# A hybrid decoder layer: output projection and norm taken in tile order 0, 1, 4, 5, 2, 3, 6, 7, with the residual transfers on SyncE, the token sums on VectorE and the norm's gains folded into the weight rows

## The chip, the cores and the metric

The kernel runs on one core of a Trainium2 chip. The metric is the device time of one execution in microseconds; for the kernel before it is the median of three runs. Five engines work side by side, each through its own list of instructions in order: TensorE (PE, matrix products), VectorE (DVE), ScalarE (ACT), GpSimd (POOL) and SyncE (SP, which only issues transfers here). An instruction waits at the head of its engine's list until what it needs is there, and everything behind it on that engine waits with it.

## The reference, cut to what matters

One layer of a decoder trunk over 1024 tokens of width 1024, all float32. The first half (projections, a state-space mixer, sparse attention, the gated merge `m` of both) is the same in both kernels. What the change touches is the end:

```python
x = x + (g_a * y_a + g_b * y_b) @ w_out[l]          # (1024 x 1024) @ (1024 x 1024)
h = rmsnorm(x, norm_ffn_g[l])
x = x + (jax.nn.silu(h @ w_ffn_gate[l]) * (h @ w_ffn_up[l])) @ w_ffn_down[l]   # 1024 -> 2816 -> 1024
return rmsnorm(x, norm_final_g)
```

## The kernel before

Every float32 operand of a product is split into a high part that TensorE takes at full rate and a low rest (`split`: ACT copies the high part, DVE subtracts), and each product is three matmuls: high by high, high by low, low by high. In the names, `wh`/`wl` are the two parts of a weight tile, `mhi`/`mlo` those of the activations.

**Merge** (`merge`). The 1024 tokens are eight tiles of 128. `w_out` is taken in units of 256 rows by 512 columns (`Weights.next`: the unit in hand has been split, the next is split now, the two behind it are loaded; two raw and three split buffers). A group of tiles shares a unit: tiles 0 to 3 first (four units for the left 512 columns, `q` = 0, and four for the right), then tiles 4 and 5, then 6 and 7, 24 units in all, each loaded and split anew. `add` adds a finished bank to the residual tile `x1`; `norm` squares and sums the row, makes the reciprocal root (`rstd`, ACT and four small DVE instructions), multiplies by it and by the gain row `gffn`, and sends `x1` to DRAM (`xd`). `turn` transposes the tile on PE. Both `x1`'s loads and its stores to `xd` are issued on ACT's queue.

**Feed-forward** (`Winograd`). Each of the 22 matrices (11 of gate, 11 of up, 256 columns each, alternating) is multiplied with the normed activations by Strassen and Winograd's seven products in place of eight, so blocks are needed that are sums of the four quarters: quarters of the contraction (2) by halves of the tokens (tiles 0 to 3, tiles 4 to 7). For the tokens these sums (`t1` to `t4`) are made in `turn` for tiles 4 to 7 against tiles 0 to 3 and kept as `T0` to `T2`; for the weights (`sums`, tile `S`) on POOL, for each matrix. A product is 12 matmuls of 512 columns. Products 1 and 2 need tokens of tiles 0 to 3 only; 3 to 7 need all eight tiles. `early` runs products 1 and 2 of matrices 0 and 1 ahead of `turn(6)` and `turn(7)`, and `run` does the rest. Results go to DRAM (`sd`).

**Down** (`down_loads`, `down`). For each half of the tokens, 22 steps: one loads a piece of the hidden layer back from `sd` (`sr`), splits it (`shi`, `slo`), splits one unit of `w_ffn_down` and does 24 matmuls. `after` is called near the end of the last matrix of `up` and issues the first loads.

The order on each engine is the order in which the Python code emits instructions; buffer counts (`bufs`) decide which of them wait.

## Time and profile before

| what | value |
|---|---|
| median of 3 runs | 1702.38 us (1698.72 to 1703.1) |
| the profiled execution, own time | 1707.91 us |
| its span | 1706.0 us |
| PE busy | 1586.6 us, 93% |
| DVE, ACT, POOL busy | 926.2, 623.7, 564.4 us |

The span is what the engines' records cover; the execution's own time is 1.91 us longer. The profiled execution is 5.5 us above the median of the runs. Merge runs from about 839 to 1009 us, the feed-forward's matrices to 1421 us and the down part from there to the end.

### The profile page before, as it was taken

To read this page: it belongs to the slowest core of one execution; us is meant where nothing else is said; L and a number is where in the kernel's file an instruction comes from. 1 tells how busy PE (TensorE), PEld (TensorE's weight loads), DVE (VectorE), ACT (ScalarE), POOL (GpSimd) and SP (SyncE) were. 2 spreads that over 40 slices of the span, in tenths; PEclk is the share of its full clock that TensorE was granted. 3 is DMA by queue.
4 is the path that set the end of the run, shared out by engine and by line. 5 is a ranking of instruction groups with operands and counts; after the bars stand their busy time and mean duration, and the time that the engine had idled before them with its cause. 6 is when DMAs were issued, how large, how long until landed. Compare 5 with 4: busy or idle time off the path is not lost.

```text
span 1706.0 us, 22111 instructions
## 1 busy us (share of the span) xinstructions
PE 1586.6 (93%) x7868; PEld 1323.6 (78%) x7868; DVE 926.2 (54%) x1735; ACT 623.7 (37%) x1266; POOL 564.4 (33%) x581
## 2 busy tenths in 40 slices
PE   8989999999998999999987659999999996999995
PEld 7667888888886998997765448888888884888884
DVE  7268776412344999997645754444444442335433
ACT  5122334202211898993123333233233331223322
POOL 1037667200120555554300445444544441000001
PEclk9999999999999999999998779999999997999998
DMA  6323443374358411104645211232222214444551
GB/s 211 112 84 109 127 136 90 96 187 115 117 146 265 109 52 47 51 2 134 212 135 192 79 56 56 81 98 87 82 85 87 74 50 131 153 172 159 193 181 60
DMA packets 164773, 196.88 MB, mean 115 GB/s; under 512 B 19770, under 2 KB 118486, under 8 KB 164663
## 3 DMA queue, kind: packets, MB, share of 16 engines
q1 hardware_dynamic: 162359, 187.08, 35.6%
q10 hardware_dynamic: 2304, 8.39, 1.3%
q8 instruction: 63, 1.03, 0.3%
q14 instruction: 47, 0.39, 0.1%
HBM read 145.48 MB, written 47.84 MB: 113 GB/s over the span
## 4 chain that ended last, share of the span: by engine, by line
PE 78%; DVE 8%; DMA 4%; ACT 3%; POOL 2%; issue 2%; SPq 1%; ACTq 0%; POOLq 0%; DVEq 0%
PE a L334 7%; PE a L336 7%; PE a L335 7%; PE a L212 5%; PE a L213 5%; PE a L214 5%; PE O L1241 3%; PE T L1223 3%; PE S L1125 3%; PE b L214 2%; PE b L212 2%; PE b L213 2%; PE a L1521 2%; PE a L1519 2%; PE a L1520 2%
## 5 line engine op out<-in xcount | busy, mean ns | idle before, releaser
L346 DVE TENSOR_TENSOR wl<-wr,wh 128x1024 fp32r<-128x1024 f32 (+1 forms) x170 | 186.2, 1109 | 139.9 <-ACT wh L343 126.9
L334 PE MATMUL a<-hhi,wh 128*128 128x512 f32 x448 | 184.9, 413 | 0.4 <-POOL wh L341 0.4
L343 ACT CAST wh<-wr 128x1024 fp32r<-128x1024 f32 (+1 forms) x138 | 113.4, 842 | 186.8 <-DMA wr<-in_w_out 42.0
L336 PE MATMUL a<-hhi,wl 128*128 128x512 f32 x448 | 178.6, 399 | 2.2 <-DVE wl L346 2.2
L335 PE MATMUL a<-hlo,wh 128*128 128x512 f32 x448 | 178.5, 398 | 0.0
L1196 POOL TENSOR_SCALAR P<-P,sum,gates 128x640 f32<-128x640 f32 (+3 forms) x192 | 124.8, 663 | 116.8 <-DVE sum L1190 70.3
L212 PE MATMUL a<-mhi,wh 128*128 128x512 f32 x352 | 138.0, 392 | 3.7 <-ACT p L225 3.7
L213 PE MATMUL a<-mlo,wh 128*128 128x512 f32 x352 | 137.8, 391 | 0.0
L214 PE MATMUL a<-mhi,wl 128*128 128x512 f32 x352 | 137.5, 391 | 0.0
L1225 DVE TENSOR_TENSOR PTl<-T,PTh 128x512 fp32r<-128x512 f32 (+3 forms) x200 | 104.2, 544 | 10.2 <-ACT PTh L1224 8.7
L341 POOL TENSOR_SCALAR wh<-wr 128x1024 fp32r<-128x1024 f32 x32 | 34.7, 1086 | 216.8 <-PE a L335 163.3
L334 PEld LDWEIGHTS a<-hhi,wh 128*128 128x128 f32 x448 | 85.9, 192 | 25.1 <-issue 6.2
L336 PEld LDWEIGHTS a<-hhi,wl 128*128 128x128 f32 x448 | 85.4, 191 | 22.9 <-DVE wl L346 2.6
L346 DVE TENSOR_TENSOR slo<-sr,shi 128x512 fp32r<-128x512 f32 x44 | 30.4, 691 | 133.3 <-ACT shi L343 133.3
L335 PEld LDWEIGHTS a<-hlo,wh 128*128 128x128 f32 x448 | 85.9, 192 | 17.9
L1176 ACT ACTIVATE P<-P,m 128x640 f32<-128x640 f32 (+7 forms) x128 | 95.8, 748 | 9.1 <-DVE m L1160 9.1
L1224 ACT CAST PTh<-T 128x512 fp32r<-128x512 f32 (+3 forms) x200 | 88.6, 476 | 21.2 <-PE T L1223 20.4
L1160 DVE CUSTOM_DVE_ANT_0 P<-S,B 128x640 f32<-128x640 f32 (+7 forms) x128 | 89.5, 700 | 4.3 <-PE S L1125 2.1
L1223 PE MATMUL T<-cst,P 128*128 128x128 f32 x592 | 87.3, 274 | 3.7 <-DVE PTl L1225 3.1
L343 ACT CAST shi<-sr 128x512 fp32r<-128x512 f32 x44 | 27.3, 620 | 170.0 <-PE c L1520 154.4
L388 POOL TENSOR_SCALAR x1f<-x1f,rstd 128x1024 f32<-128x1024 f32 (+1 forms) x2 | 2.3, 1142 | 251.8 <-DVE rstd L368 246.5
L1519 PE MATMUL a<-wh,shi 128*128 128x512 f32 x176 | 71.0, 403 | 15.4 <-issue 13.6
(411 smaller groups left out, 4017.8 us busy)
## 6 DMA issues: line engine op xcount, KB each, us to landing
wr<-in_w_ffn_down SPq DMA_DIRECT2D x44, 512.0 KB, 3.4
wr<-in_w_in SPq DMA_DIRECT2D x28, 512.0 KB, 4.3
wr<-in_w_out SPq DMA_DIRECT2D x24, 512.0 KB, 5.2
wr<-in_w_ffn_gate SPq DMA_DIRECT2D x22, 512.0 KB, 5.2
wr<-in_w_ffn_up SPq DMA_DIRECT2D x22, 512.0 KB, 4.5
sr<-sd SPq DMA_DIRECT2D x44, 256.0 KB, 3.7
gd<-evf SPq DMA_DIRECT2D x32, 256.0 KB, 2.1
Q<-qd SPq DMA_DIRECT2D x64, 128.0 KB, 3.0
```

What stands on the lines that cost most here:

```text
L212: mm(ps, wh[:, k], bh[:, k], start=first and k == 0, stop=False, skip_group_check=True)
L213: mm(ps, wh[:, k], bl[:, k], start=False, stop=False, skip_group_check=True)
L214: mm(ps, wl[:, k], bh[:, k], start=False, stop=k == 3, skip_group_check=True)
L334: mm(ps, a, c, start=start and k == 0, stop=False, skip_group_check=True)
L335: mm(ps, a, d, start=False, stop=False, skip_group_check=True)
L336: mm(ps, b, c, start=False, stop=stop and k == nk - 1, skip_group_check=True)
L343: nc.scalar.copy(hi, src)
L346: (nc.gpsimd if lo_eng == "pool" else nc.vector).tensor_tensor(lo, src, hi, op=OP.subtract)
L1196: sc = lambda x, y, z: GP.tensor_scalar(x, x, a[:, y:y + 1], gate(z), op0=OP.mult, op1=OP.mult)
L1223: T.transpose(t[:, x, :], p[:, c:c + P], self.ident)
L1225: V.tensor_tensor(ol, t[:, 0:len(cc), :], oh, op=OP.subtract)
L1519: mm(ps, hi[:, t], wh[:, 0, col], start=f == 0, stop=False)
```

## The change

Tiles are taken as 0, 1, 4, 5 (four tiles share each of eight units), then 2, 3, 6, 7 for the left columns (four units), then 2, 3 and 6, 7 apart for the right columns (four units each): 20 units in place of 24. `x1` is loaded and stored from SP. The squares follow the add directly, and a tile's reciprocal root and scaling (now one ACT copy with a scale) come one tile later. The gain vector is no longer multiplied into each row: POOL multiplies it into the weight rows of every matrix (`scale`, eight instructions of 128x256 in place, ahead of `sums`), from a column tile `gcol` (`factors`). The token sums of `turn`, some on POOL before, are on DVE, and for tiles 6 and 7 they are cut into pieces that stand between the products of matrix 0 (`first`). `after` is cut into three steps at earlier places of the last matrix. The core of the diff (`broadcast_row` of `gffn` is dropped, and the old loop of `merge` too):

```diff
+        self.fresh[n] = ts
         self.r[n] = lambda i, k: ts[k - 1][:, :, P * (i - 1):P * i]
+    def scale(self, n):
+        for kh, t in enumerate(self.fresh.pop(n, ())):
+            for k in range(4):
+                self.K.nc.gpsimd.tensor_scalar(t[:, k], t[:, k], self.g[:, 4 * kh + k:4 * kh + k + 1], 1.0,
+                                               op0=OP.mult, op1=OP.mult)
+    def factors(self):
+        self.K.nc.sync.dma_start(self.g, self.K.A["norm_ffn_g"].rearrange("(k p) -> p k", p=P))
+        self.K.nc.gpsimd.tensor_scalar(self.g, self.g, -0.5, 1.0, op0=OP.mult, op1=OP.mult)
...
         if n >= len(self.mats):
             return
+        self.scale(n)
         GP, A = self.K.nc.gpsimd, self.r[n]
...
-    def early(self):
-        self.sums(0)
+    def first(self, turn):
+        V, GP = self.K.nc.vector, self.K.nc.gpsimd
         self.p1(0)
+        self.t2(0)
         self.p1(1)
+        turn("transpose", 6)
+        turn("T1", 6)
         self.p2(0)
+        turn("transpose", 7)
+        turn("T1", 7)
+        self.t3(0)
         self.p2(1)
+        z5, z3, v, y, c = (self.K.bank(t) for t in "aabbc")
+        self.product(0, 5, z5)
+        turn("B22", 6)
+        turn("B22", 7)
+        self.t4(0)
+        self.load(2)
+        self.product(0, 3, z3)
+        turn("T3", 6)
+        turn("T3", 7)
+        self.product(0, 7, v)
+        turn("T2", 6)
+        turn("T2", 7)
+        self.product(0, 6, y)
+        turn("T4", 6)
+        turn("T4", 7)
+        u2, p5, u3 = self.p.pop(0), self.tile("p1"), self.tile("x11")
+        self.K.nc.scalar.copy(p5, z5)
+        V.tensor_tensor(u2, u2, y, op=OP.add)
+        V.tensor_tensor(u3, u2, v, op=OP.add)
+        V.tensor_tensor(u2, u2, z3, op=OP.add)
+        self.sums(1)
+        self.t2(1)
+        self.product(0, 4, c)
+        GP.tensor_tensor(u2, u2, p5, op=OP.add)
+        GP.tensor_tensor(p5, u3, p5, op=OP.add)
+        self.out(0, 1, 1, p5)
+        self.out(0, 0, 1, u2)
+        V.tensor_tensor(u3, u3, c, op=OP.add)
+        self.out(0, 1, 0, u3)
...
+        if last:
+            next(self.after)
         z = K.bank("a")
         self.product(n, 5, z)
         p5 = self.tile("p5")
         AC.copy(p5, z)
-        if n:
-            self.t1(n + 1)
+        self.t1(n + 1)
...
+        self.t2(n + 1)
         if last:
-            self.after()
-        self.t2(n + 1)
+            next(self.after)
         c = K.bank("c")
         self.product(n, 4, c)
...
-        self.t2(0)
-        for n in range(len(self.mats)):
+        for n in range(1, len(self.mats)):
...
         def load(tt):
             x1[tt] = pool.tile([P, D], F32, name="x1", tag="x1", bufs=4)
-            nc.scalar.dma_start(x1[tt], self.A["x"][P * tt:P * tt + P, :])
+            nc.sync.dma_start(x1[tt], self.A["x"][P * tt:P * tt + P, :])
+        def unit(u, q):
+            return self.W.next("w_out", 256 * u, 2, 512 * q, 512, ("act", "dve"))
         def part(w, u, tt, o):
             t = slice(P * tt, P * tt + P)
         def add(tt, q, o):
             x = x1[tt][:, 512 * q:512 * q + 512]
             V.tensor_tensor(x, x, o, op=OP.add)
+            if q:
+                sq[tt] = pool.tile([P, 1], F32, name="ss", tag="ss", bufs=4)
+                xns[tt] = pool.tile([P, D], F32, name="xn", tag="xn", bufs=4)
+                AC.activation(xns[tt], x1[tt], AF.Square, accum_out=sq[tt])
+                nc.sync.dma_start(xd[tt], x1[tt])
         def norm(tt):
-            xns[tt] = self.norm(pool, x1[tt], g, "xn", "dve", 2)
-            nc.scalar.dma_start(xd[tt], x1.pop(tt))
-        def turn(tt):
+            AC.activation(xns[tt], x1.pop(tt), AF.Copy, scale=self.rstd(pool, sq.pop(tt)))
...
+            if what == "T1":
+                pb, pc = (p.rearrange("p (k t) -> p k t", k=4) for p in ps.pop(tt))
+                b22, t1, t3 = tmp[tt] = [pool.tile([P, 4, P], F32, name=n, tag=n, bufs=2)
+                                         for n in ("b22", "t1", "t3")]
+                AC.copy(b22, pc)
+                V.tensor_tensor(t1, pb, first(0, 0), op=OP.subtract)
+                V.tensor_tensor(t1, t1, first(1, 0), op=OP.subtract)
+                V.tensor_tensor(t3, b22, pb, op=OP.subtract)
+                x, o = t1, [x[:, 0:4, at] for x in m]
+            else:
+                b22, t1, t3 = tmp[tt]
+            if what == "B22":
+                x, o = b22, [x[:, 4:8, at] for x in m]
+            elif what == "T3":
+                x, o = t3, [x[:, :, c] for x in td[1]]
+            elif what == "T2":
+                V.tensor_tensor(t1, b22, t1, op=OP.subtract)
+                x, o = t1, [x[:, :, c] for x in td[0]]
+            elif what == "T4":
+                V.tensor_tensor(t3, first(0, 1), t1, op=OP.subtract)
+                V.tensor_tensor(t3, t3, first(1, 1), op=OP.add)
+                x, o = t3, [x[:, :, c] for x in td[2]]
+            self.split(*o, x, "act", "dve")
+        def turned(tt):
             if tt < 4:
                 self.transposed("bc", xns.pop(tt), m[0], m[1], tt)
-                return
-            xs, ps = xns.pop(tt), [self.bank(t) for t in "bc"]
-            for h in range(2):
-                for k in range(4):
-                    nc.tensor.transpose(ps[h][:, k * P:k * P + P], xs[:, (4 * h + k) * P:(4 * h + k + 1) * P],
...
-            V.tensor_tensor(t1, pb, first(0, 0), op=OP.subtract)
-            AC.copy(b22, pc)
-            GP.tensor_tensor(t1, t1, first(1, 0), op=OP.subtract)
-            V.tensor_tensor(t3, b22, pb, op=OP.subtract)
-            GP.tensor_tensor(t2, b22, t1, op=OP.subtract)
-            GP.tensor_tensor(t4, first(0, 1), t2, op=OP.subtract)
-            GP.tensor_tensor(t4, t4, first(1, 1), op=OP.add)
...
+        def units(tts, q, between):
+            banks = [self.bank("a") for _ in tts]
+            for u in range(4):
+                w = unit(u, q)
+                for f, *a in between.get((u, "w"), ()):
+                    f(*a)
+                for i, tt in enumerate(tts):
+                    part(w, u, tt, banks[i])
+                    if u == 3:
+                        add(tt, q, banks[i])
+                        if q and i:
+                            norm(tts[i - 1])
+                for f, *a in between.get(u, ()):
+                    f(*a)
+        units((0, 1, 4, 5), 0, {(0, "w"): [(load, tt) for tt in (0, 1, 4, 5)] + [(ffn.factors,)]})
+        units((0, 1, 4, 5), 1, {3: [(norm, 5)]})
+        units((2, 3, 6, 7), 0, {0: [(turned, 0)], 1: [(turned, 1), (turned, 4)],
+                                (1, "w"): [(load, 2), (load, 3)], (2, "w"): [(load, 6), (load, 7)],
+                                2: [(turned, 5)], (3, "w"): [(ffn.load, 0)], 3: [(ffn.sums, 0)]})
+        units((2, 3), 1, {3: [(norm, 3)]})
+        units((6, 7), 1, {1: [(turned, 2)], (2, "w"): [(ffn.load, 1)], 2: [(turned, 3), (ffn.t1, 0)],
+                          (3, "w"): [(ffn.scale, 1), (ffn.t1, 1)], 3: [(norm, 7)]})
+        ffn.first(turn)
...
         def after():
+            loads[2](2)
             W.until(None)
+            W.ahead(0, 2)
+            yield
+            W.ahead(1, 2)
+            loads[3](1)
+            yield
             W.ahead(2, 4)
-            loads[3](1)
-        ffn.run(after)
+            loads[3](2)
+            yield
+        ffn.run(after())
         for p in (ffn.late, fp, rp, tp, mp):
             p.release()
         pool = self.pool("dn")
```

Three places in the instruction order carry the prediction. The first is ACT at the end of the first group's right columns. Before, tiles 0 to 3 (`x_8706` is tile 0's residual, `xd_8692` its place in DRAM, `x_8992` tile 4's):

```order
L343 CAST wh<-wr 128x1024 x8
L376 ACTIVATE xn,ss<-x_8706 128x1024
L360 ACT_TABLE_LOAD
L360 ACTIVATE rstd<-ss,eps 128x1
L1385 DMA xd_8692<-x_8706 128x1024
L376 ACTIVATE xn,ss<-x_8708 128x1024
L360 ACTIVATE rstd<-ss,eps 128x1
L1385 DMA xd_8693<-x_8708 128x1024
L1369 DMA x_8992<-in_x 128x1024
L1369 DMA x_8994<-in_x 128x1024
L343 CAST wh<-wr 128x1024
```

Now, tiles 0, 1, 4, 5 (`x_8714` to `x_8720`):

```order
L1441 ACTIVATE xn,ss<-x_8714 128x1024
L1441 ACTIVATE xn,ss<-x_8716 128x1024
L413 ACT_TABLE_LOAD
L413 ACTIVATE rstd<-ss,eps 128x1
L1445 ACTIVATE xn<-x_8714,rstd 128x1024
L1441 ACTIVATE xn,ss<-x_8718 128x1024
L413 ACTIVATE rstd<-ss,eps 128x1
L1445 ACTIVATE xn<-x_8716,rstd 128x1024
L1441 ACTIVATE xn,ss<-x_8720 128x1024
L413 ACTIVATE rstd<-ss,eps 128x1
L1445 ACTIVATE xn<-x_8718,rstd 128x1024
L413 ACTIVATE rstd<-ss,eps 128x1
```

The transfers are gone from ACT's list; all four tiles' squares, roots and scaled copies now stand ahead of the next unit's `wh`, where two tiles' squares and roots stood.

The second is SP's list at the last matrix of up and the first down loads. Before (`sd_8688` to `sd_8691` are the last matrix's four results):

```order
L247 DMA sd_8688<-x_12406 128x512
L235 DMA sd_8691<-p_12426 128x512
L235 DMA sd_8689<-p_12378 128x512
L94 DMA wr<-in_w_ffn_down 128x1024 x4
L1469 DMA sr<-sd_8648 128x512
L235 DMA sd_8690<-u_12441 128x512
L351 DMA gfin<-in_norm_final_g 128x1024
L1469 DMA sr<-sd_8650 128x512
```

Now:

```order
L262 DMA sd_8688<-x_12552 128x512
L1523 DMA sr<-sd_8648 128x512
L1523 DMA sr<-sd_8650 128x512
L94 DMA wr<-in_w_ffn_down 128x1024 x2
L250 DMA sd_8691<-p_12580 128x512
L250 DMA sd_8689<-p_12524 128x512
L94 DMA wr<-in_w_ffn_down 128x1024 x2
L250 DMA sd_8690<-u_12603 128x512
L404 DMA gfin<-in_norm_final_g 128x1024
L1523 DMA sr<-sd_8652 128x512
```

The first two pieces of the hidden layer and the first two units of `w_ffn_down` now stand ahead of three of the last matrix's four stores; the third and fourth unit stand between them, and the third piece behind them all.

The third is POOL in the middle of the feed-forward, one matrix of gate. Before (`p_9913` and `u_9934` are its result tiles):

```order
L189 TENSOR_TENSOR S<-wr 128x512
L190 TENSOR_TENSOR S<-S,wr 128x512
L191 TENSOR_TENSOR S<-wr 128x512
L192 TENSOR_TENSOR S<-wr,S 128x512
L279 TENSOR_TENSOR p_9913<-u_9934,p_9913 128x512
```

Now:

```order
L171 TENSOR_SCALAR wr<-wr,gcol 128x256 x8
L204 TENSOR_TENSOR S<-wr 128x512
L205 TENSOR_TENSOR S<-S,wr 128x512
L206 TENSOR_TENSOR S<-wr 128x512
L207 TENSOR_TENSOR S<-wr,S 128x512
L333 TENSOR_TENSOR p_10055<-u_10076,p_10055 128x512
```

Eight instructions are new for each of the 22 matrices, ahead of the four sums.

## Rows read from the trace of the kernel before

**Rows 1.** By stretch: length; busy PE, PEld, DVE, ACT, POOL; PE's clock, DMA share, GB/s.

```profile
876.00:1040.60 164.60, 112.89 (x443) 87.10 (x442) 99.02 (x124) 61.19 (x94) 48.23 (x32) 0.84 0.33 107
1041.00:1421.40 380.40, 380.40 (x1679) 314.78 (x1678) 160.75 (x188) 116.90 (x177) 170.86 (x127) 1.00 0.25 78
1421.40:1452.00 30.60, 15.21 (x50) 11.38 (x50) 8.08 (x9) 6.49 (x9) 2.32 (x2) 0.72 0.57 188
```

**Rows 2.** Waits of PE, 876 to 1041 us: releaser, total us, times, longest.

```profile
PE a L1375 <- ACT wh L343: 23.2, 6, 5.8
PE b L212 <- ACT wh L343: 16.1, 1, 16.1
PE a L1376 <- DVE wl L346: 7.3, 8, 2.0
```

**Rows 3.** PE's timeline: start, us, line, tiles, [idle before <- releaser].

```profile
845.34 0.39 PE L1375 MATMUL a<-wh,mhi 128*128 128x512 f32 x1
...
875.96 0.39 PE L1375 MATMUL a<-wh,mhi 128*128 128x512 f32 x1
...
883.84 0.60 PE L397 MATMUL b<-cst,xn 128*128 128x128 f32 x4
...
1009.22 0.80 PE L212 MATMUL b<-T0h,wh 128*128 128x512 f32 x1 [16.11 <-ACT wh L343]
...
1014.91 0.63 PE L212 MATMUL a<-mhi,wh 128*128 128x512 f32 x1
```

**Rows 4.** ACT by shape, 870 to 1010 us: busy, mean ns | idle before, releasers.

```profile
L343 ACT CAST wh<-wr 128x1024 fp32r<-128x1024 f32 x16 | 16.5, 1047 | 29.3 <-DMA xd<-x 13.0 <-DMA wr<-in_w_out 12.2 <-PE a L1377 3.9
L376 ACT ACTIVATE xn<-x 128x1024 f32<-128x1024 f32 x8 | 8.5, 1062 | 17.7 <-DVE x L1381 17.7
...
L360 ACT ACTIVATE rstd<-ss,eps 128x1 f32<-128x1 f32 x8 | 2.4, 295 | 0.2
...
L360 ACT ACT_TABLE_LOAD x1 | 1.3, 1283 | 0.0
```

**Rows 5.** DVE by shape, 870 to 1010 us, columns as in group 4.

```profile
L1381 DVE TENSOR_TENSOR x<-x,a 128x512 f32<-128x512 f32 x12 | 8.1, 684 | 8.7 <-PE a L1377 8.6
L346 DVE TENSOR_TENSOR T1l<-t,T1h 128x512 fp32r<-128x512 f32 x4 | 7.0, 1752 | 0.0
...
L402 DVE TENSOR_TENSOR mlo<-b,mhi 128x512 fp32r<-128x512 f32 x4 | 2.7, 686 | 0.4 <-ACT mhi L401 0.4
...
L364 DVE SCALAR_TENSOR_TENSOR rstd<-rstd 128x1 f32<-128x1 f32 x8 | 1.8, 219 | 0.3
...
L346 DVE TENSOR_TENSOR wl<-S,wh 128x1024 fp32r<-128x1024 f32 x1 | 1.2, 1226 | 0.3 <-ACT wh L343 0.3
```

**Rows 6.** POOL by shape: the sums in 1041 to 1421 us.

```profile
L191 POOL TENSOR_TENSOR S<-wr 128x512 f32<-128x512 f32 x19 | 24.5, 1291 | 0.0
```

**Rows 7.** POOL by shape, whole span: instructions with a scalar read for each partition.

```profile
L1196 POOL TENSOR_SCALAR P<-P,sum,gates 128x256 f32<-128x256 f32 x16 | 8.9, 557 | 0.0
...
L388 POOL TENSOR_SCALAR x1f<-x1f,rstd 128x512 f32<-128x512 f32 x1 | 1.2, 1172 | 5.3 <-ACT rstd L360 5.3
L388 POOL TENSOR_SCALAR x1f<-x1f,rstd 128x1024 f32<-128x1024 f32 x1 | 1.1, 1112 | 246.5 <-DVE rstd L368 246.5
```

**Rows 8.** Transfers: issuing queue, count, KB each, median us from issue to landing.

```profile
wr<-in_w_out SPq DMA_DIRECT2D x24, 512.0 KB, 5.2
```

**Rows 9.** Timeline at the start of the down part: SP's issues, then PE.

```profile
1421.38 7.80 SPq L94 DMA_DIRECT2D wr<-in_w_ffn_down  x4
1429.23 0.42 SPq L1469 DMA_DIRECT2D sr<-sd  x1
1437.82 0.33 SPq L235 DMA_DIRECT2D sd<-u  x1
...
1435.22 0.77 PE L1519 MATMUL a<-wh,shi 128*128 128x512 f32 x1 [13.65 <-issue]
...
1451.91 0.39 PE L1519 MATMUL a<-wh,shi 128*128 128x512 f32 x1
```

More of the change, by code (lines that the diff above doesn't have):

```diff
@@ L144, in __init__ @@
         self.K, self.raw, self.pool, self.sd, self.late = K, raw, pool, sd, None
+        self.g = pool.tile([P, KD], F32, name="gcol")
+        self.fresh = {}
         f = lambda j, h: [x[:, 4 * j:4 * j + 4, 512 * h:512 * h + 512] for x in m]
@@ L272, in rest @@
         AC.copy(p5, z)
-        if n:
-            self.t1(n + 1)
+        self.t1(n + 1)
+        if last:
+            next(self.after)
         v = K.bank("b")
@@ L283, in rest @@
         self.out(n, 0, 1, u2)
+        self.t2(n + 1)
         if last:
-            self.after()
-        self.t2(n + 1)
+            next(self.after)
         c = K.bank("c")
@@ new lines, in norm, with turn @@
+        def norm(tt):
+            AC.activation(xns[tt], x1.pop(tt), AF.Copy, scale=self.rstd(pool, sq.pop(tt)))
+        def turn(what, tt):
+            at, c = slice(P * tt, P * tt + P), slice(P * (tt - 4), P * (tt - 4) + P)
+            first = lambda i, j: m[i][:, 4 * j:4 * j + 4, c].bitcast(F32)
+            if what == "transpose":
+                xs, ps[tt] = xns.pop(tt), [self.bank(t) for t in "bc"]
+                for h in range(2):
+                    for k in range(4):
+                        nc.tensor.transpose(ps[tt][h][:, k * P:k * P + P],
+                                            xs[:, (4 * h + k) * P:(4 * h + k + 1) * P], self.ident)
+                return
+            if what == "T1":
[21 more added lines that the diff above has]
+            self.split(*o, x, "act", "dve")
@@ L1397, in turn @@
-            at, c = slice(P * tt, P * tt + P), slice(P * (tt - 4), P * (tt - 4) + P)
-            first = lambda i, j: m[i][:, 4 * j:4 * j + 4, c].bitcast(F32)
-            v = lambda n: pool.tile([P, 4, P], F32, name=n, tag=n, bufs=1)
-            t1, t2, t3, t4, b22 = (v(n) for n in ("t1", "t2", "t3", "t4", "b22"))
-            V.tensor_tensor(t1, pb, first(0, 0), op=OP.subtract)
-            AC.copy(b22, pc)
-            GP.tensor_tensor(t1, t1, first(1, 0), op=OP.subtract)
-            V.tensor_tensor(t3, b22, pb, op=OP.subtract)
@@ L1415, in merge @@
-        unit = lambda u, q: self.W.next("w_out", 256 * u, 2, 512 * q, 512, ("act", "dve"))
-        for tt in range(4):
-            load(tt)
-        for q in range(2):
-            banks = [self.bank("a") for _ in range(4)]
+            else:
+                for what in ("transpose", "T1", "B22", "T3", "T2", "T4"):
+                    turn(what, tt)
+        def units(tts, q, between):
+            banks = [self.bank("a") for _ in tts]
             for u in range(4):
                 w = unit(u, q)
-                for tt in range(4):
-                    part(w, u, tt, banks[tt])
+                for f, *a in between.get((u, "w"), ()):
+                    f(*a)
+                for i, tt in enumerate(tts):
+                    part(w, u, tt, banks[i])
@@ L1424, in merge @@
                     if u == 3:
-                        add(tt, q, banks[tt])
-                        if q and tt < 2:
-                            norm(tt)
-        load(4)
-        load(5)
-        for first in (4, 6):
-            for q in range(2):
-                banks = [self.bank("a") for _ in range(2)]
-                for u in range(4):
-                    w = unit(u, q)
-                    last = first == 6 and q == 1
-                    if last and u >= 2:
-                        if u == 2:
-                            ffn.load(1)
-                        ffn.t1(u - 2)
-                    for i in range(2):
-                        tt = first + i
-                        part(w, u, tt, banks[i])
-                        if u == 3:
-                            add(tt, q, banks[i])
-                            if q:
-                                norm(tt)
-                    if first == 4 and q == 0:
-                        turn(u)
-                        if u < 2:
-                            norm(u + 2)
-                            load(u + 6)
-                    if first == 6 and q == 0 and u % 2:
-                        turn(4 + u // 2)
-                    if first == 6 and q == 0 and u == 0:
-                        ffn.load(0)
@@ L1456, in merge @@
-        ffn.early()
-        turn(6)
-        turn(7)
+                        add(tt, q, banks[i])
[8 more added lines that the diff above has]
+                                2: [(turned, 5)], (3, "w"): [(ffn.load, 0)], 3: [(ffn.sums, 0)]})
```

13 lines of the change are left out of this document (2 added, 11 removed).

## The prediction

> **What bounds the kernel now.** I read the busy time by stretch first. From 1041 to 1421 us, the feed-forward's matrices, PE is busy all the time at its full clock [rows 1]: nothing that the change does to other engines can shorten it, and it can only be hurt there. In the stretch before, 876 to 1040.6 us, PE is busy 112.9 of 164.6 us, and at a mean clock of 0.84, so part of that is matmuls at half speed; in the 30.6 us behind 1421.4 it is busy half the time [rows 1]. These two stretches are where a change to the merge and to the first down loads can gain.
>
> How much is lost there? A matmul of 512 columns starts every 0.227 us at full clock: 135 of them lie between the two starts at 845.34 and 875.96 [rows 3], counted in threes of one line each. From 875.96 (the last unit of tiles 0 to 3) to 1040.6 PE has, by the code, one unit for four tiles (24 matmuls), 16 units for two tiles (192) and the 14 products of matrices 0 and 1 (168): 384 by 0.227 = 87 us, and 64 transposes, for which I take 7 us (0.60 us for four at most, overlapping [rows 3]). 164.6 - 94 leaves **70.6 us lost**. At the start of the down part two steps of 24 matmuls need 10.9 us, but the third begins at 1451.91 [rows 3, 9], 30.5 us after 1421.4: **19.6 us lost**.
>
> The waits of PE say on whom: ACT's `wh` for 23.2 us in six waits and for 16.1 in one, DVE's `wl` for 7.3 [rows 2]. The one of 16.1 ends at 1009.22 [rows 3]: it is the tail behind `turn(6)` and `turn(7)`. ACT in turn had waited 13.0 us behind stores of `xd`, with `wh` next in its list, and 12.2 us for the weight to land [rows 4].
>
> **What the change removes and what stays late.** PE's work stays the same (384 matmuls, 64 transposes): four tiles at 24 matmuls a unit in place of two at 12. So the question is only how much of the 70.6 us remains. I laid the new order out on each engine from the start of unit 7 (time 0; units count 0 to 19), with these prices: unit `wh` 1.05 us and `wl` 1.23; a square or a scaled copy 1.06 each, the square's read-out 0.19 (an estimate from the small operations beside it), a root 0.30 and the table load 1.28; DVE on 128x512 0.69, with 0.61 between starts; the reciprocal root's trip through DVE 0.75, three dependent instructions of up to 0.22 [rows 4, 5]; a unit of `w_out` lands 4.3 us after its issue, between 3.6 and the 5.2 of the median, which holds the crowded start too [rows 8].
>
> (a) *End of the first group.* ACT has four squares (5.0), a table load (1.3), four roots (1.2), four scaled copies (4.2) and four trips to DVE (3.0), some 14.7 us in a row, and they begin at 2.4. `wh` of unit 9 stands behind them: 18.2. PE has unit 7, unit 8 and tile 0's transposes, free at 11.8. Lost 6.4, and 0.8 for `wl`: 7.2.
> (b), (c) *Tiles 4 and 5.* One `turned` is 11 instructions on DVE and two trips to ACT, 8.6 us behind its transposes. The next unit's `wh` and `wl` stand behind it, 2.3 more, against PE's 6.3 for a unit and a tile's transposes. With the `mlo` of tile 1 ahead, 4.2 is lost before unit 11 and 3.9 before unit 12. Moving the token sums from POOL to DVE buys little here: 1.75 us for a subtraction beside POOL [rows 5] goes, but four more instructions come.
> (d) *Units 13 to 16*, two tiles each, 2.7 us of PE. Two units circle through two raw buffers: issue, 4.3 to land, `wh`, `wl`, about 7.2 for two, 3.6 each; beside POOL's `scale` and `sums` of matrix 0 `wl` is slower. Lost 2.9.
> (e) *Unit 17* stands behind the norms of tiles 2 and 3: 5.5.
> (f) *Transposes of tile 6.* The second half of matrix 1's weights waits for the raw buffer that unit 19's split frees, lands 4.3 later, is scaled on POOL, and `t1(1)` takes it on ACT ahead of the squares of 6 and 7. Products 1 of both matrices cover 5.4 of it. Lost 5.5.
> (g) *The pieces of tiles 6 and 7* between the products of matrix 0. DVE has 22 instructions there and 11 others against five products of 2.7 us: lost 1.3, 2.6, 0.2, 1.3 and 2.5 before products 5, 3, 7, 6 and 4, and 1.3 before product 7 of matrix 1. In this, the four `sums` of matrix 1 cost DVE about 4 us at 1.75 for 0.69 [rows 5].
> (h) *Clock.* After the wait of 16.1 us the matmuls run at the half clock to 1014.91, 0.63 where 0.39 is usual [rows 3], 13 of them at 0.2 more each. Five of the waits above are over 3 us; I take 1.5 each: 7.5.
>
> Sum 7.2 + 8.1 + 2.9 + 5.5 + 5.5 + 9.2 + 7.5 = **46 us still lost**, 24.6 gained. With 3.6 or 5.2 us for a landing it is 44 or 48; with 0.7 to 3 us for the clock, 42 to 53; my prices for the trips between engines can be wrong by a tenth of the chains, 5 either way: 38 to 56.
>
> (SBUF's shared port: the Trainium skill, "SBUF — State Buffer", section "SBUF: two separate sides", says that a GpSimd instruction that reads SBUF and a DVE instruction with two SBUF inputs lock each other out for a whole instruction. The row of 1.752 us beside POOL against 0.686 [rows 5] agrees that they collide. It speaks against moving sums to DVE while POOL gets more to do: by a full lock the four sums would hold DVE for 5.2 us, not 4, and (g) would lose 1 us more.)
>
> **The factors on POOL.** 22 x 8 instructions of 128x256. One with two scalars of this size takes 0.557 us, one with a single scalar on four times the columns 1.112, so 0.28 to 0.56; a crowded one on twice the columns took 1.172, the far bound [rows 7]. I take 0.5, nearest to the row of the same size: 4 us a matrix. A matrix is 84 matmuls, 19.0 us of PE, and POOL is busy 170.9 of 380.4 us, 8.5 a matrix [rows 1]: 12.5 with the factors. What hides them is that the products of the matrix before run meanwhile: `scale` and `sums` together are 9.2 us (4, and four of 1.29 [rows 6]) and are wanted by `t1` about 11 and by `t2` about 16 us into it. Cost nothing. The gain row's load, now 1024 single elements ahead of the units from 4 on, has 15 us before they are wanted; bound from below nothing, from above a few us inside that slack. The loads of `x1` on SP stand ahead of the same units: nothing too. Without that cover each would cost its landing.
>
> **The down part.** Before, the first piece is issued at 1429.23, after four weight loads (begun at 1421.38) of which two wait for splits, and the second only after the store at 1437.82, which waits for POOL and DVE [rows 9]. Now two pieces and two units are issued when product 2 of the last matrix is done, some 10 us before 1421.4, and split before it: step one starts at once, step two too. Late next is the third piece: it is issued behind the store of the last result (about 1427), lands 5 to 6 us later, and its split and `wh` (1.7) follow, while PE wants it at 1432.3. That is 1.5 to 5 us, with the clock; I take 3.5. **16 us gained**, 13 to 19.6 as bounds.
>
> **Sum.** 24.6 + 16 = 40.6. The profiled execution takes 1707.9, so 1667.3 of its own; it lies 5.5 above the median, so against 1702.4 the forecast is **1662 us**. Bounds: 14.6 + 13 = 28 to 32.6 + 19.6 = 52: 1650 to 1674. The prices of the laid-out chains come from one execution and the order has many small waits, so I widen by 5: 1645 to 1679.
>
> **Rivals.**
> *The norm chains hold PE as long as before.* The four-tile chain in (a) is longer than the two-tile one it replaces, and DVE gets work. If the waits in (a) to (g) are half as long again (38 to 57), with the clock 66 are lost, and only the down part gains: 1702 - 5 - 16 = 1681. For it: 8.6 us on DVE per tile is what `turn` took before. Against it: the single wait of 16.1 has products to fill it. Chance 0.11.
> *Nearly all hidden.* ACT no longer stands behind stores (13.0 us [rows 4]), and if landings are short and the clock does not fall, 25 us remain: 1702 - 46 - 18 = 1638. Chance 0.08.
> *POOL and DVE's two-input work become the bound of the feed-forward.* If the collision of a subtraction with POOL [rows 5] were complete, 8.5 us of POOL, the factors and DVE's splits (two of 1.23, three of 0.69: 4.5) would have to fit one behind another into 19.0 us: with 0.75 us for a factor they would just do, and with 1.172 it is 22.4, 3.4 over, 20 times: 68 lost, 1702 - 41 + 68 = 1729. It decides from 1.0 us a factor, where the loss meets the gain. The page of the Trainium skill named above states such a lock. Against: nothing crowded it to 1.0 in the row of 0.557. Chance 0.04.
> *The change does not do what it says in the down part* (the third piece costs all that was won): 1662 + 13 = 1675, inside the range.
>
> **Chances.** Forecast 0.77, the three rivals 0.11, 0.08, 0.04. The range 1645 to 1679 leaves out the three. About 0.3% (5 us) is what a measurement here can tell. The first two rivals are faster too; the third is slower by more than that in most of its span, the rest is no change: faster 0.95, same 0.02, slower 0.03.
>
> **What would show it.** Right: from unit 7 to the end of matrix 1 some 140 us in place of 164.6, with waits for `wh` at units 9, 11, 12 and 17 of 3 to 6 us each, none of 16; a wait at the transposes of tile 6; no idle at the start of the down part and a wait of some us at its third step; no gap in the matrices behind the second. Wrong: idle PE at each matrix with `wh` late behind POOL's factors; `wh` of unit 9 before 15 us; a wait at step one of the down part.

## The result and the profile after

The changed kernel takes 1659.12 us (median of four runs, 1658.18 to 1663.42) against 1702.56 us for the kernel before in the same session: a ratio of 0.9755 with a 95% interval of 0.9732 to 0.9777, 43.4 us less. Its profiled execution has a span of 1656.2 us, 49.8 less than that of before.

Where did it come from? I cut both executions at three matmuls: the first of the merge (unit 0), the first of product 4 of matrix 1, and the last of the feed-forward. Busy time by stretch (columns as in [rows 1]), first before, then after:

```profile
831.51:1037.89 206.38, 151.90 (x606) 118.61 (x604) 111.85 (x139) 68.45 (x101) 49.24 (x33) 0.87 0.36 119
1037.89:1421.18 383.29, 383.29 (x1692) 317.38 (x1691) 163.44 (x189) 118.33 (x178) 173.89 (x129) 1.00 0.25 78
1421.18:1706.00 284.82, 250.69 (x1058) 200.29 (x1056) 109.56 (x148) 82.84 (x121) 8.20 (x6) 0.94 0.45 155
```

```profile
826.70:1000.75 174.05, 147.71 (x605) 116.52 (x604) 96.94 (x143) 70.37 (x104) 38.27 (x40) 0.90 0.38 126
1000.75:1384.05 383.30, 383.30 (x1693) 317.68 (x1692) 174.81 (x191) 121.21 (x182) 256.47 (x280) 1.00 0.26 81
1384.05:1656.20 272.15, 249.13 (x1058) 201.19 (x1056) 109.60 (x147) 79.67 (x117) 13.34 (x9) 0.96 0.45 158
```

The merge became 32.3 us shorter, the matrices stayed as they were (383.29 and 383.30, with POOL's busy time up from 173.89 to 256.47), the down part became 12.7 shorter: 45.0 in all. The other 4.8 us of the 49.8 are ahead of unit 0, where nothing was changed: over all profiled executions of this study unit 0 begins between 826.70 and 832.90. Alone this moves an execution by up to 6 us, so below the stretches from unit 0 stand beside the medians.

Inside the merge, counted from unit 7 to the end of matrix 1:

```profile
874.60:1040.60 166.00, 114.29 (x449) 88.26 (x448) 99.02 (x124) 61.19 (x94) 48.23 (x32) 0.85 0.33 107
```

```profile
864.80:1003.47 138.67, 112.33 (x449) 87.21 (x448) 83.23 (x128) 64.08 (x98) 37.28 (x39) 0.88 0.33 113
```

The first is before, the second after. (Unit 7 of before begins at 874.60, six matmuls ahead of the row that the forecast took for its start.) PE's own work is 94 us in both, as the prediction counted it. So PE idled 51.7 us before and 26.3 after, and was busy 20.3 and 18.3 us longer than those 94. Most of that, not all, is the clock. After, the granted clock stood at 0.50 (1.2 GHz in place of 2.4) in six places; from PE's first matmul there to the end of each, columns as above for PE, its clock and the DMA:

```profile
882.14:888.13 5.99, 5.52 (x12) 0.50 0.42 124
902.34:908.61 6.27, 5.81 (x13) 0.50 0.58 198
915.44:918.85 3.41, 3.41 (x10) 0.50 1.01 324
934.94:939.33 4.39, 3.92 (x8) 0.50 0.45 116
956.40:963.23 6.83, 6.27 (x19) 0.50 0.00 0
973.47:976.88 3.41, 3.41 (x10) 0.50 0.39 119
```

That is 28.3 us of busy time at half the clock, of which half, some 14 us, is lost; before, it was 31.2 us, so some 16. The other 4 to 5 us are not clock: part of them is that the last matmul ahead of a wait is booked with 0.39 us, where in an unbroken run the next one starts 0.227 behind it. So the merge's gain from unit 7 on is idle time (25.4 us); the clock gave back little.

PE's timeline of after shows the waits that are left, which answer to [rows 2, 3]:

```profile
875.56 0.50 PE L1431 MATMUL a<-wh,mhi 128*128 128x512 f32 x1 [1.07 <-DVE rstd L414]
882.14 0.79 PE L1431 MATMUL a<-wh,mhi 128*128 128x512 f32 x1 [4.05 <-ACT wh L396]
883.40 0.80 PE L1432 MATMUL a<-wl,mhi 128*128 128x512 f32 x1 [0.47 <-DVE wl L399]
...
902.34 0.80 PE L1431 MATMUL a<-wh,mhi 128*128 128x512 f32 x1 [3.17 <-ACT wh L396]
...
914.36 0.47 PE L1431 MATMUL a<-wh,mhi 128*128 128x512 f32 x1 [2.90 <-DVE x L1437]
...
934.94 0.79 PE L1431 MATMUL a<-wh,mhi 128*128 128x512 f32 x1 [4.71 <-ACT wh L396]
...
956.29 1.06 PE L1455 MATMUL b<-cst,xn 128*128 128x128 f32 x4 [3.15 <-ACT xn L1445]
958.77 0.80 PE L227 MATMUL a<-mhi,wh 128*128 128x512 f32 x1 [0.56 <-ACT p L240]
...
972.32 0.50 PE L228 MATMUL a<-mlo,wh 128*128 128x512 f32 x1 [1.89 <-DVE mlo L399]
...
984.95 0.49 PE L227 MATMUL c<-T2h,wh 128*128 128x512 f32 x1 [1.89 <-ACT T2h L396]
...
1400.16 0.79 PE L1573 MATMUL a<-wh,shi 128*128 128x512 f32 x1 [4.56 <-ACT wh L396]
```

In order: the bank of tile 5, units 9 (two rows), 11, 12 and 17, the transposes of tile 6, product 2 of matrix 0, products 3 and 4, the third step of the down part. At unit 12 PE waits for an add on DVE that frees a bank, not for `wh`; that add starts at 913.53, behind the pieces of tile 5 in DVE's list. The wait of 16.11 is gone. The first step of the down part begins at 1384.28, right behind the last product, where [rows 9] show 1435.22 for a last product at 1421.18.

A gain that the prediction had not seen lies ahead of unit 7: from unit 0 to unit 7 it is 874.60 - 831.51 = 43.1 us before and 864.80 - 826.70 = 38.1 after, 5.0 less. The timeline of before shows it at unit 1 (ACT, then PE), and a second place of the same kind:

```profile
835.87 2.16 ACTq L1369 DMA_DIRECT2D x<-in_x  x4
838.07 1.99 ACT L343 CAST wh<-wr 128x1024 fp32r<-128x1024 f32 x2 [24.49 <-PE a L1377]
...
839.17 0.49 PE L1375 MATMUL a<-wh,mhi 128*128 128x512 f32 x1 [2.01 <-ACT wh L343]
840.43 0.50 PE L1376 MATMUL a<-wl,mhi 128*128 128x512 f32 x1 [0.77 <-DVE wl L346]
...
890.02 0.33 ACTq L1385 DMA_DIRECT2D xd<-x  x1
894.92 0.33 ACTq L1369 DMA_DIRECT2D x<-in_x  x1
895.30 1.04 ACT L343 CAST wh<-wr 128x1024 fp32r<-128x1024 f32 x1 [5.00 <-DMA xd<-x]
```

The four loads of `x` head ACT's list and go out at 835.87; `wh` of units 1 and 2 stands behind them, and PE waits. The last three rows correct a reading of [rows 4]: the 13.0 us that ACT waited "behind stores" are a *load* that waits at ACT's head until the store of the same buffer has landed. The store itself takes ACT no time that shows.

### The profile page after: what moved, and what is told of

Read it like the earlier page. It is cut to its first block, busy times and chain, and to the rows that moved or that the text cites. A ratio compares the mean times of both kernels' runs of the same rounds, so it can differ in the third digit from the quotient of the medians.

```text
span 1656.2 us, 22268 instructions
## 1 busy us (share of the span) xinstructions
PE 1578.5 (95%) x7868; PEld 1322.2 (80%) x7868; DVE 922.4 (56%) x1739; ACT 626.2 (38%) x1270; POOL 641.2 (39%) x742
## 3 DMA queue, kind: packets, MB, share of 16 engines
q8 instruction: 63, 1.03, 0.3%
## 4 chain that ended last, share of the span: by engine, by line
PE 83%; DVE 6%; ACT 3%; DMA 3%; issue 2%; POOL 1%; SPq 1%; POOLq 0%; ACTq 0%; DVEq 0%
PE a L387 7%; PE a L389 7%; PE a L388 7%; PE a L227 5%; PE a L228 5%; PE a L229 5%; PE O L1294 4%; PE T L1276 3%; PE S L1178 3%; PE a L1574 2%; PE a L1575 2%; PE a L1573 2%; PE b L229 2%; PE b L227 2%; PE b L228 2%
## 5 line engine op out<-in xcount | busy, mean ns | idle before, releaser
L399 DVE TENSOR_TENSOR wl<-wr,wh 128x1024 fp32r<-128x1024 f32 (+1 forms) x166 | 193.4, 1177 | 126.7 <-ACT wh L396 107.1
L396 ACT CAST wh<-wr 128x1024 fp32r<-128x1024 f32 (+1 forms) x134 | 109.7, 837 | 157.1 <-DMA wr<-in_w_out 48.9
L171 POOL TENSOR_SCALAR wr<-wr,gcol 128x256 f32<-128x256 f32 x176 | 93.1, 548 | 91.8 <-DMA wr<-in_w_ffn_gate 77.0
L388 PEld LDWEIGHTS a<-hlo,wh 128*128 128x128 f32 x448 | 85.9, 192 | 17.6
L1277 ACT CAST PTh<-T 128x512 fp32r<-128x512 f32 (+3 forms) x200 | 88.4, 475 | 21.4 <-PE T L1276 20.6
L399 DVE TENSOR_TENSOR wl<-S,wh 128x1024 fp32r<-128x1024 f32 x44 | 66.4, 1510 | 41.4 <-ACT wh L396 41.4
```

The costliest lines, as they stand in the source:

```text
L388: mm(ps, a, d, start=False, stop=False, skip_group_check=True)
L396: nc.scalar.copy(hi, src)
L399: (nc.gpsimd if lo_eng == "pool" else nc.vector).tensor_tensor(lo, src, hi, op=OP.subtract)
```

## The experiments

All are edits of the changed kernel; "merge" is the stretch from unit 0 to product 4 of matrix 1 (174.05 us in the changed kernel), "down" that behind the last product (272.15). Merges scatter: in the changed kernel and in the four runs whose edit leaves the merge alone or costs it nothing by the median (`x` on ACT in its new place, `xd` on ACT, and two of the down part), they take 173.76 to 175.84 us. Unless said otherwise the rest was as in the changed kernel.

**The first four loads of `x` ahead of unit 0, on ACT**, and the same loads on ACT in their new place (the first two lines of the diff alone).

```diff
-            nc.sync.dma_start(x1[tt], self.A["x"][P * tt:P * tt + P, :])
+            (nc.scalar if tt in (0, 1, 4, 5) else nc.sync).dma_start(x1[tt], ...)
...
+        for tt in (0, 1, 4, 5):
+            load(tt)
-        units((0, 1, 4, 5), 0, {(0, "w"): [(load, tt) for tt in (0, 1, 4, 5)] + [(ffn.factors,)]})
+        units((0, 1, 4, 5), 0, {(0, "w"): [(ffn.factors,)]})
```

> The changed kernel with its first four loads of `x` back where they stood before: on ACT, ahead of unit 0. Theory (ACT's order at the start of the merge): in the profile of before the four loads begin at 835.87 on ACT, `wh` of units 1 and 2 stands behind them until 838.07, PE waits 2.01 and 0.77 us at unit 1 and then runs 8 or so matmuls at the half clock; from unit 0 to unit 7 PE takes 44.5 us before (831.51 to 875.96, whatever the unit's row) against 38.1 after. So this kernel gives 5 to 6.5 us back: 1664 to 1666 us, with that wait at unit 1 in its trace. Rival (the difference lay between two executions, the loads cost nothing): 1657 to 1661, no wait at unit 1.

> The changed kernel with the first four loads of `x` issued by ACT again, but in their new place, behind unit 0's weight. Theory (the place in the order counts, not the queue): `wh` of unit 1 now stands ahead of the loads, only unit 2's can be held, and PE wants that about 11 us after unit 0's start: 0 to 1 us, 1658 to 1661. Rival (ACT's queue is what costs): as much as with the loads ahead of unit 0, 1664 to 1666.

Measured: 1664.55 us (ratio 0.9777, 0.9755 to 0.9799) and 1659.8 (0.975, 0.9732 to 0.9768). PE's timeline of the first:

```profile
838.98 0.50 PE L1431 MATMUL a<-wh,mhi 128*128 128x512 f32 x1 [1.67 <-ACT wh L396]
840.24 0.50 PE L1432 MATMUL a<-wl,mhi 128*128 128x512 f32 x1 [0.76 <-DVE wl L399]
```

The wait at unit 1 is back with the first and absent with the second, where the row of tile 5's bank comes 48.85 us behind unit 0 (48.86 in the changed kernel, 51.87 in the first edit). So the place in ACT's list costs 3.0 us, and ACT's queue nothing. The median (5.4 above the changed kernel's) lies in the expectation, but unit 0 of the profiled execution began 5.0 late; by the stretch it is less than 5 to 6.5. One reason is that the clock stayed at 1.00 here up to unit 7 and was 0.96 on average in before, where it fell behind this wait; another that the 44.5 us of the expectation end six matmuls into unit 7.

**The stores of `xd` on ACT again.**

```diff
-                nc.sync.dma_start(xd[tt], x1[tt])
...
+            nc.scalar.dma_start(xd[tt], x1.pop(tt))
```

> The changed kernel with the stores of `xd` issued by ACT again, each behind the scaled copy of its tile. Theory (a store costs ACT its issue alone, some 0.54 us as the four loads at 835.87 took 2.16): the chain at the end of the first group grows by 2 us, that of tiles 2 and 3 by 1, that of 6 and 7 by 1, all of it in front of `wh`: 1662 to 1664. Rival (ACT stands behind stores for as long as before, 13.0 us): 1668 to 1673, with ACT's waits for `xd` in the trace. Second rival (the chains are not what PE waits for): 1657 to 1661.

Measured: 1660.63 us (0.9759, 0.9737 to 0.9781), merge 173.76: nothing, and the wait at unit 9 is 4.05 as it was. My theory of 0.54 us a store was wrong: the store's row starts with the scaled copy's, at 878.11, and the next instruction follows at 879.17 at once. With the rows at 890.02 to 895.30 above this leaves the reloads as what held ACT before. The reloads of tiles 2, 3, 6 and 7 from ACT weren't tried.

**The down part in one step.**

```diff
         def after():
-            loads[2](2)
-            W.until(None)
-            W.ahead(0, 2)
             yield
-            W.ahead(1, 2)
-            loads[3](1)
             yield
+            W.until(None)
             W.ahead(2, 4)
-            loads[3](2)
+            loads[3](1)
             yield
```

> The changed kernel with the start of the down part as before: its first piece and its weights in one step, behind the second result of the last matrix. Theory: the step of the forecast was worth 16 us; the two profiles show 30.5 us from the end of the products to the third step before and 16.1 after, and 1.7 us at the half clock more behind it after: 12.7. So 1671 to 1673, by the forecast's size 1675. Rival (the third piece is late in any case and takes back what the first two win): 1659 to 1663.

Measured: 1671.73 us (0.9814, 0.9792 to 0.9836), 12.6 above the changed kernel; down 282.74, 10.6 more. PE waits 13.03 us at 1398.28 for the first piece. The new steps are worth 11 to 13 us, not 16.

**POOL's factors twice.**

```diff
                 self.K.nc.gpsimd.tensor_scalar(t[:, k], t[:, k], self.g[:, 4 * kh + k:4 * kh + k + 1], 1.0, ...
+                self.K.nc.gpsimd.tensor_scalar(t[:, k], t[:, k], 1.0, 1.0, op0=OP.mult, op1=OP.mult)
```

> The changed kernel with each of POOL's factors followed by a second one of the same size that multiplies by one. Theory (hidden): `scale` grows from some 4.2 to 8.3 us a matrix, and with the sums to about 14.2; the products of the matrix before take 19.0, and `t1` wants the rows about 11 us into them, `t2` the sums about 16. So nothing in matrices 2 to 21; at matrix 1, whose scaling is not covered as well, 2 to 6 us once: 1659 to 1666. Rival (POOL and DVE's two-input work shut each other out): 12.5 and 4.2 of POOL and 4.5 of DVE do not fit into 19.0 us, 2.2 over in each of 20 matrices: some 1700.

Measured: 1680.5 us (0.9879, 0.9858 to 0.99), 21.4 more: neither. Its matrices and four rows of PE's timeline:

```profile
1005.65:1405.97 400.32, 390.91 (x1692) 316.76 (x1691) 197.90 (x192) 121.02 (x183) 351.85 (x434) 1.00 0.24 78
```

```profile
1015.50 0.50 PE L228 MATMUL a<-mhi,wh 128*128 128x512 f32 x1 [1.53 <-ACT p L241]
1035.73 0.79 PE L228 MATMUL b<-T0h,wh 128*128 128x512 f32 x1 [3.62 <-ACT wh L397]
...
1115.44 0.50 PE L230 MATMUL b<-T0h,wl 128*128 128x512 f32 x1 [0.41 <-DVE wl L400]
...
1154.60 0.50 PE L230 MATMUL b<-T0h,wl 128*128 128x512 f32 x1 [0.37 <-DVE wl L400]
```

The merge is 4.0 longer (178.01), the matrices 17.0. POOL is busy 351.85 of 400.32 us, 17.6 a matrix. Two matrices take 39.2 us (1115.44 to 1154.60) in place of 38.1. The product that is late is the one whose weights come from the sums (`t2`), but the sums were not what it waited for. POOL's and ACT's rows ahead of 1154.60:

```profile
1148.57 1.29 POOL L208 TENSOR_TENSOR S<-wr,S 128x512 f32<-128x512 f32 x1
1149.82 1.27 POOL L334 TENSOR_TENSOR p<-u,p 128x512 f32<-128x512 f32 x1
1151.12 1.15 ACT L247 ACTIVATE p<-p 128x512 f32<-128x512 f32 x2 [6.56 <-POOL p L334]
1152.18 1.04 ACT L397 CAST wh<-S 128x1024 fp32r<-128x1024 f32 x1
```

The two sums that `t2` reads are done at 1146.90. Behind the four sums stands the addition of a result (`p`, line 334) on POOL; ACT waits for it with two activations of gate, and `wh` of the sums stands behind these on ACT. In the changed kernel POOL idles 1.9 us ahead of this addition in a matrix of gate and 4.6 in one of up, and there is no wait of PE. So one factor is hidden and two are not, and the place where the cover ends is POOL's addition of the result and ACT's activations behind it, which the expectation (and the prediction, with its 11 and 16 us) left out.

**The token sums on POOL** (four instructions of `turn`, from `V` to `nc.gpsimd`).

```diff
-                V.tensor_tensor(t1, t1, first(1, 0), op=OP.subtract)
+                nc.gpsimd.tensor_tensor(t1, t1, first(1, 0), op=OP.subtract)
...
```

> The changed kernel with the four token sums of each of tiles 4 to 7 that were on POOL back on POOL. Theory (the chain counts): a subtraction takes 1.29 us there and 0.69 on DVE, and each adds a trip to another engine of 0.2 to 0.3 us; DVE beside POOL slows down. `turned` grows by 3 us for tiles 4 and 5, and the pieces of 6 and 7 by as much: 6 to 10 us, 1665 to 1669. Rival (DVE's number of instructions counts, and four a tile fewer set it free): 1655 to 1659.

Measured: 1660.86 us (0.9764, 0.9741 to 0.9787), merge 176.48, 2.4 longer, little more than the scatter.

```profile
904.67 0.79 PE L1431 MATMUL a<-wh,mhi 128*128 128x512 f32 x1 [4.89 <-ACT wh L396]
...
918.42 0.76 PE L1431 MATMUL a<-wh,mhi 128*128 128x512 f32 x1 [5.61 <-DVE x L1437]
...
974.47 0.50 PE L228 MATMUL a<-mlo,wh 128*128 128x512 f32 x1 [0.51 <-DVE mlo L399]
...
986.64 0.50 PE L227 MATMUL c<-T2h,wh 128*128 128x512 f32 x1 [0.48 <-ACT T2h L396]
```

Both were half right. For tiles 4 and 5, one chain, the waits grow by 1.7 and 2.7 us (3.17 and 2.90 above); for tiles 6 and 7, two chains side by side, DVE's number of instructions counts and the waits at products 3 and 4 shrink from 1.89 each to about half a microsecond. Moving the sums is worth little in sum.

**All of tile 6, then all of tile 7.**

```diff
-        turn("transpose", 6)
-        turn("T1", 6)
+        for what in ("transpose", "T1", "B22", "T3", "T2", "T4"):
+            turn(what, 6)
...
```

> The changed kernel with all pieces of tile 6 made at once and then all of tile 7, in place of piece by piece; the products keep their order. Theory: the first piece of tile 7 comes some 8 us later, so that the first product that needs both tiles starts at about 975 in place of 967, and the four others follow without waits where they now lose about 4: a loss of 3 to 6 us, 1662 to 1665. Rival (the last piece comes when it came, and that alone sets the end): 1658 to 1660.

Measured: 1663.61 us (0.9778, 0.9754 to 0.9802), merge 177.50, 3.5 longer. The first product that needs both tiles waits 4.29 us at 973.20, and the waits of 1.89 are gone: as the theory had it.

**The old tile groups**: 0 to 3, then 4 and 5, then 6 and 7.

```diff
-        units((0, 1, 4, 5), 0, ...
+        units((0, 1, 2, 3), 0, ...
+        units((0, 1, 2, 3), 1, {3: [(norm, 3)]})
+        units((4, 5), 0, {0: [(turned, 0)], 1: [(turned, 1)], ..., 2: [(turned, 2)], ..., 3: [(turned, 3)]})
+        units((4, 5), 1, {3: [(norm, 5)]})
+        units((6, 7), 0, {..., 1: [(turned, 4)], 3: [(turned, 5), (ffn.sums, 0)]})
...
```

> The changed kernel with the tiles in their old groups: 0 to 3, then 4 and 5, then 6 and 7, and everything else as changed. Theory: the same matmuls in 24 units, 16 of them of two tiles (2.7 us of PE); the two pieces of work of 8.6 us on DVE for tiles 4 and 5 stand beside units of 2.7 in place of 5.4, and the norms of 4 and 5 get a stall of their own: 10 to 15 us lost, 1669 to 1675. Rival (the order is worth little, the gain of the merge came from the pieces between the products and from ACT's list): 1659 to 1663.

Measured: 1674.89 us (0.9844, 0.9817 to 0.987), merge 188.87, 14.8 longer.

```profile
884.00 0.80 PE L1431 MATMUL a<-wh,mhi 128*128 128x512 f32 x1 [7.93 <-ACT wh L396]
...
919.41 0.80 PE L1431 MATMUL a<-wh,mhi 128*128 128x512 f32 x1 [4.98 <-ACT wh L396]
...
936.73 0.79 PE L1431 MATMUL a<-wh,mhi 128*128 128x512 f32 x1 [7.38 <-ACT wh L396]
...
953.08 0.80 PE L1431 MATMUL a<-wh,mhi 128*128 128x512 f32 x1 [5.97 <-ACT wh L396]
```

The same chains stand beside units of half the length, and one norm chain more. The order is the largest single piece of the merge's gain that was tried, nearly half of 32.3. Of the rest the place of `x` gave 3.0; what the squares, the scaled copies and the missing reloads on ACT gave apart was not tried.

**Three edits that let a late instruction come sooner**, alone and together. The first piece is units 9 and 17, the second the split of matrix 1's second half behind the norms (`half` is one half of `t1`), the third the down part.

```diff
-                        if q and i:
+                        if q and i and tts[0] != 2:
...
+        units((0, 1, 4, 5), 1, {(3, "w"): [(self.W.ahead, 2, 3)], 3: [(norm, 5)]})
+        units((2, 3), 1, {3: [(self.W.ahead, 2, 3), (norm, 2), (norm, 3)]})
...
+                          (3, "w"): [(ffn.scale, 1), (ffn.half, 1, 0)], 3: [(norm, 7), (ffn.half, 1, 1)]})
...
-            loads[2](2)
+            loads[2](4)
             W.until(None)
             W.ahead(0, 2)
             yield
-            W.ahead(1, 2)
             loads[3](1)
+            W.ahead(1, 3)
+            loads[3](2)
             yield
             W.ahead(2, 4)
-            loads[3](2)
+            loads[3](3)
             yield
```

> The changed kernel with the split of unit 9 ahead of the norms of the first group, and that of unit 17 between the squares and the roots of tiles 2 and 3. Theory (the waits at units 9 and 17 are those of `wh` behind the norms' chain on ACT): 4.05 and 0.47 us and 4.71 and 0.47 go, and with each some 2.6 us at the half clock: up to 14.9, less what is late next (the pieces of tiles 4 and 5 on DVE begin 4 to 5 us sooner, but their length stays): 8 to 13 us, 1646 to 1651. Rival (PE would wait for the transposes' inputs at the same places in any case): 1656 to 1659.

> The changed kernel with the second half of `t1` of matrix 1, which waits for POOL's factors, split behind the norms of tiles 6 and 7 in place of ahead of them. Theory (the transposes of tile 6 wait because the adds and squares of 6 and 7 stand behind that split): 3.15 and 0.56 us and about 2.5 at the half clock go: 4 to 6 us, 1653 to 1655. Rival (the pieces of tiles 6 and 7 on DVE set the end of the products in any case): 1657 to 1660.

> The changed kernel with the loads of the third and fourth piece of the down part issued with the first two, and the third weight's load ahead of the last matrix's stores on SP. Theory (the third step waits for its piece, whose load stands behind those stores): the wait of 4.56 and 0.47 us goes, and the half clock behind it: 6 to 8 us, 1651 to 1653. Rival (the third weight, which needs a buffer that the first one's split sets free, is then as late): 1656 to 1659.

> The three edits together: units 9 and 17 split sooner, the second half of `t1` of matrix 1 later, the third and fourth piece of the down part loaded sooner. Theory (the waits are one behind another, so their gains add): 18 to 27 us, 1632 to 1641. Rival (one wait is given back at the next place: the pieces of tiles 4 to 7 on DVE): half of it, 1645 to 1650.

| edit | median, ratio (interval) | merge | down |
|---|---|---|---|
| units 9 and 17 | 1651.95, 0.9699 (0.9682 to 0.9715) | 164.79 | 272.8 |
| half of `t1` | 1660.62, 0.9753 (0.9736 to 0.9769) | 171.70 | 271.4 |
| down part | 1655.35, 0.9725 (0.9711 to 0.9739) | 174.2 | 265.32 |
| together | 1641.76, 0.9643 (0.9628 to 0.9658) | 162.25 | 264.65 |

The waits at unit 9 are gone and that at unit 17 is 1.04: 9.3 us of the merge, inside the theory's 8 to 13; the median shows 7.2, and unit 0 of its profiled execution began 3.0 late. In the down part the wait at the third step is gone: 6.8 us by its stretch, inside 6 to 8; the median shows 3.8, and unit 0 began 4.0 late. With the half of `t1` the wait of 3.15 at the transposes goes, and these come in its place:

```profile
960.31 0.50 PE L236 MATMUL a<-mhi,wh 128*128 128x512 f32 x1 [1.91 <-ACT p L249]
...
973.27 0.50 PE L237 MATMUL a<-mlo,wh 128*128 128x512 f32 x1 [2.00 <-DVE mlo L408]
...
977.27 0.50 PE L237 MATMUL b<-T1l,wh 128*128 128x512 f32 x1 [0.97 <-DVE T1l L408]
```

Of these the 0.97 stands as 0.99 in the run of the old down part too, which leaves the merge alone. PE idles 26.0 us in this kernel's stretch from unit 7 against 26.3. The merge is 2.4 us shorter, and 2.5 shorter in the run of all edits than in that of units 9 and 17, hardly more than the scatter, and the median shows no gain: nearer to the rival than to 4 to 6 us. Together the edits are 17.4 us faster than the changed kernel, just under the 18 expected, and the fastest kernel of this study: 60.98 us below the kernel before in its session (1702.74).

## Why the prediction was right, and which of its terms were not

The forecast of 1662 us is 2.9 above the median, and each sign it named came: 138.67 us from unit 7 to the end of matrix 1 (some 140 forecast), waits of 3 to 5 us at units 9, 11, 12 and 17 (that at unit 12, 2.90, for an add on DVE where `wh` was named), one at the transposes of tile 6, none of 16, no gap in the matrices behind the second, an immediate start of the down part and a late third step. But that the sum came within 3 us is in part luck, because errors of both signs met in it:

- *The chains, (a) to (g)*: 38.4 us of idle PE forecast, 26.3 measured. (a) 7.2 against 5.6 with the bank of tile 5; (b) and (c) 8.1 against 6.5; (e) 5.5 against 5.2 (each with its wait for `wl`): the chain of instructions on ACT and DVE was laid out rightly and a little long. `wh` of unit 9 ended 17.3 us behind unit 7's start, for 18.2. (d), the load circle of units 13 to 16, is missing from the trace: 2.9 against nothing. Its landing of 4.3 us had no row behind it: where the trace of before has a unit's landing, it took 3.82 to 7.05. (f) 5.5 against 3.7, and in the half-of-`t1` run, which removes it, PE idles as long, with the time back in (g). (g) 9.2 against 5.1.
- *(h), the clock*: 7.5 forecast, some 14 measured, and another 4 us in which PE was busy beyond the 94 without the clock. This is the term with the largest error. The row of before already hinted at it: 112.89 us busy for 94 of work [rows 1]. I had subtracted one sum from the other and called all of it lost, without parting idle time from slow time, and then priced a wait at 1.5 us of half clock where [rows 3] gave 13 matmuls at 0.2 more each, 2.6: five waits at that price are 13.
- *The start of the merge*: "nothing" forecast, 5.0 us measured, of which the run with the loads ahead of unit 0 gave 3.0 back. The step "the loads of `x1` on SP ... nothing too" looked at what stood behind the loads in their new list, not at what had stood behind them in the old one.
- *The factors*: nothing, as forecast (0.54 us each for 0.5), and some 12.8 us of POOL a matrix (256.47 by 20) for the 12.5 worked out. The rival that had POOL and DVE as the bound put its turning point at 1.0 us a factor; two factors, some 1.03 us, cost 21 us where the gain is 43, so that its price was too high. (SBUF's lock: the Trainium skill, "SBUF — State Buffer", section "SBUF: two separate sides", lets a VectorE instruction with two SBUF inputs and a GpSimd instruction that reads SBUF block each other for a whole instruction. The rows around 970 us at the end of this text agree that the two collide, but a pair goes through in 1.55 to 1.70 us, less than the 1.98 of one behind the other.) The matrices of 383.29 and 383.30 us show no price for one factor. The cover was argued with the wrong due time, that of the sums; what two factors made late is POOL's addition of a result.
- *The down part*: 16 forecast, 12.7 measured by the stretches, 10.6 (stretch) and 12.6 (median) by undoing it. The third step waits 4.56 us and then runs at the half clock up to about 1407: the 3.5 left over were too few. Its piece was issued at 1391.61, 7.3 us behind the last product where the forecast had 5.6, and its split began at 1398.54, 6.9 later for a landing of 5 to 6.

Of the two rivals with a chance of 0.11 and 0.08, the first (the chains hold PE as long as before) fell with an idle time halved, the second (25 us lost) with 44.6 lost (26.3 idle, 18.3 busy beyond the 94); the edits of units 9 and 17 and of `t1` together bring it to 32.9 (126.87 us from unit 7).

## What to carry to other kernels

Part a stretch's loss into idle time and slow time before pricing anything: both stand in one row, and most of the longer waits here brought some of the second with them. For work that is to be hidden on an engine, look at everything that stands behind it on that engine, not only at what reads its result. For every instruction that is moved, ask what it held up in the list that it leaves, a load that waits for a buffer above all. Put a short instruction that another engine waits for ahead of a long chain that nobody waits for yet; edits of that kind, with loads issued sooner, were worth another 17.4 us here, where the whole change had brought 43.4.
